# A decoder layer on one core: each feed-forward stage in three SBUF regions, its plain chunks first, and fixed PSUM banks

## The chip, the cores and the metric

The kernel runs on one core of one Trainium2 chip. The metric is device time in microseconds (us) of one execution. Profiles are of single executions; all times inside a trace count from the start of its span.

## What is computed

One layer of a hybrid decoder, batch 1, 256 tokens, model width 2048, all in float32:

```python
x = layer_norm(ALPHA * x + 0.5 * swiglu(x, ffn1_w_in, ffn1_w_out), ...)   # stage ffn1
z = x @ mix_w_in                                                          # stage hgrn
...                                                                       # convolution and gated recurrence
merged = sigmoid(gate_conv) * (y_conv @ branch_w_conv) + sigmoid(gate_hgrn) * (y_hgrn @ branch_w_hgrn)
x = layer_norm(ALPHA * x + merged @ mix_w_out, ...)                       # stage merge
x = layer_norm(ALPHA * x + 0.5 * swiglu(x, ffn2_w_in, ffn2_w_out), ...)   # stage ffn2
x = layer_norm(ALPHA * x + sigmoid(x @ ple_w_gate) * (p @ ple_w_proj), ...)  # stage ple
def swiglu(x, w_in, w_out):
    a, u = split(x @ w_in, 2); return (silu(a) * u) @ w_out
```

The hidden width of a feed-forward stage is 5504: ten chunks of 512 and one of 384.

## The kernel before

**Products.** Every float32 matrix product is made of three passes of TensorE (PE). A weight tile `raw` of 2x128 rows and 512 columns (512 KB) comes from HBM; ScalarE (ACT) rounds it to `wh` (the cast L884), VectorE (DVE) subtracts to get the rest `wl` (L895). Activations are split likewise into `xh`, `xl` (helper `halves`, L242 and L243). The passes wh·xh, wl·xh and wh·xl (L951 to L953) add up in a PSUM bank `acc`. Before they can be split, activations are transposed on PE into a PSUM tile `tp` (L232). A pair (`wh`, `wl`) is used for both token halves, t = 0 and t = 1.

**Units and quads.** A `Unit` is one block of 512 output columns: it goes over the inner dimension in blocks and through both token halves. A chunk of a feed-forward stage needs two units (gate and up columns). A chunk of full width can instead be a `Quad`: both column blocks and both token halves together by a scheme with seven instead of eight block products, in 2 steps; part of its weights are sums of loaded tiles, which DVE makes (L878) in a second ring of loads, `sraw`. A quad needs seven PSUM banks, `p1` to `p7`, and sums and differences of the plain transposed activations `yT`, made once by `sums` (`sh`, `sl`). In each feed-forward stage chunk 0 and the narrow chunk 10 are units, chunks 1 to 9 are quads. The chunks go in parts of 2, 2, 2, 2 and 3; after each chunk of a part from the second on come two output units of the part before (product with `w_out`), and the last four output units come at the end.

**What sets the order.** `feed` runs each time a pair has been used up: it starts loads as long as the rings have room (4 `raw`, 5 `sraw`), then casts and splits. 6 pairs are held, and more in a stage where EXTRA says so. Loads go through the queue of SyncE (SP) in the order in which they are written. `defer` runs a piece of code some ticks later, a tick being one pair's use for one token half. The instructions so written are then ordered for each engine by the framework's scheduler, which works from times of its own; each engine works through its list in that order.

**Regions.** `open_region(kind)` opens a stage's own memory: a pool on the left for its tiles, a pool `high` on the right for `sraw` and `yT`, and, where the numbers of banks differ (BANKS), new PSUM pools: 7 banks for accumulators and 1 for transposes in the feed-forward stages, else 4 accumulators, 2 for transposes and 2 for the recurrence.

**Between stages.** `layer_norm` (statistics, the square root L327 on ACT, four normalising operations L378 on DVE, transposes, then four ACT operations L370 that apply gain and bias into `y` or `yT`, then the split) stands between the stages: 8 operands, one for each of 4 columns blocks (c) and 2 token halves. Gain and bias are applied to `x` itself later (`affine_rows`, L353 and L354), at 40 to 100 ticks, with two loads `gb` into a slot of the `raw` ring.

**The start.** All eight loads of `x` are queued first with four of weights between them; then all eight transposes, each followed by its split and by an ACT copy to `yT` (L930), are written ahead of the first product.

Of the kernel before, what the change touches and what calls it, by code (L numbers as in the profile page):

```python
# [10 lines left out]
F32 = mybir.dt.float32  # L11
# [19 lines left out]
LONG = (12, 4)  # L31
EXTRA = {"ffn1": 0, "hgrn": 0, "merge": 0, "ffn2": 0, "ple": 1}
NSRAW = 5
BANKS = {"ffn1": (7, 1, 0), "ffn2": (7, 1, 0)}
ALPHA = 2.0 ** 0.25
# [71 lines left out]
def hybrid_layer(ctx: ExitStack, tc: tile.TileContext, x, p, ln_g, ln_b, ffn1_w_in, ffn1_w_out, mix_w_in,  # L107
# [16 lines left out]
    held = {}  # L124

    def open_region(kind):

        if "ctx" in region:
            region.pop("ctx").close()
        region["ctx"] = ExitStack()  # L130
        region["kind"] = kind
        held.update(sraw=0, freed=0)
        region["pool"] = region["ctx"].enter_context(tc.tile_pool(name=kind, bufs=1, side="left", reuse_waits="tile"))
        region["high"] = region["ctx"].enter_context(tc.tile_pool(name=kind + "h", bufs=1, side="right", reuse_waits="tile"))
        banks = BANKS.get(kind, (4, 2, 2))
        if banks != region.get("banks"):
            if "psum" in region:
                region["psum"].close()
            region["psum"] = ExitStack()
            region["banks"] = banks  # L140
            for n, b in zip("ath", banks):
                if b:
                    region[n] = region["psum"].enter_context(
                        tc.tile_pool(name="ps_" + n, bufs=b, space=PSUM, reuse_waits="tile"))

    def rtile(shape, dtype=F32, **kw):
        return region["pool"].tile(shape, dtype, **kw)

    def ptile(kind, name):
        return region[kind].tile([P, CC], F32, tag="bank", name=name)  # L150

# [7 lines left out]
    def defer(delay, fn):  # L159
        insort(later, (state["tick"] + delay, fn), key=lambda e: e[0])  # L160
# [67 lines left out]

    def transposed(src, nb, kind="t"):
        tp = ptile(kind, "tp")  # L230
        for i in range(nb):
            state["turned"] = nc.tensor.transpose(tp[:, i * P : (i + 1) * P], src[:, i * P : (i + 1) * P], ident).ins  # L232
        return tp
# [44 lines left out]
    def sums(stat):  # L278
# [30 lines left out]
        for i, fn in enumerate((third, first, second, fourth, lambda: delta(2), lambda: delta(3))):  # L309
            defer(2 + 2 * i, fn)  # L310

# [47 lines left out]
    def layer_norm(t, i, scale, stat):  # L359
# [3 lines left out]
        def operand(c, xc):  # L363
            y = plain_tile(t, c) if stat is x2 else st.tile([P, CC], F32, tag="silu", name="y", bufs=2)
            tp = transposed(xc, 4, "a" if stat is x2 else "t")
            if t == 0 and c < 2:
                gate["pe"] = state["turned"], 1
            for a in range(4):
                k = i * 16 + 4 * c + a
                nc.scalar.activation(y[:, a * P : (a + 1) * P], tp[:, a * P : (a + 1) * P], AF.Identity,  # L370
                                     bias=gbT[:, 48 + k : 49 + k], scale=gbT[:, k : k + 1])
# [555 lines left out]
    def first_operand(t, c):  # L927
        tp = transposed(xt[t][:, c * CC : (c + 1) * CC], 4, "a")
        halves(x0, t, c, tp, 4, "x")
        nc.scalar.copy(plain_tile(t, c), tp)  # L930
        if (t, c) == (NT - 1, 3):
            sums(x0)

    for c in range(4):
        for t in range(NT):
            load_x(t, c)
            defer(0, lambda t=t, c=c: first_operand(t, c))
            if c < 2:
                weight_dma()
# [98 lines left out]
```

## Time and profile before

| | us |
|---|---|
| median of 3 runs | 2266.34 (2264.94 to 2268.58) |
| profiled execution, its own time | 2265.55 |
| its span, first to last instruction | 2263.8 |
| busy PE, DVE, ACT within the span | 2215.5, 1682.0, 1130.7 |

The mean granted clock of TensorE was 0.992. A busy PE is not a PE at its peak: matmuls overlap, and their ends are modelled. For PE the number of instructions in a stretch tells more than the busy time: 128x512 matmuls that follow each other without a wait start about 0.23 us apart.

### The profile page before, as it was taken

The numbers are of one execution on the slowest core, as the hardware profiler recorded it, in microseconds if no ns is written. First come the engines' busy times: TensorE is split into PE (matmuls) and PEld (weight loads), VectorE is DVE, ScalarE is ACT, GpSimd is POOL, SyncE is SP. The second block draws the span as 40 slices with busy tenths as digits, with TensorE's granted clock in tenths as the row PEclk, the third lists the DMA queues.
The fourth block names the chain that finished last, engine by engine and source line by source line (L and its number), as shares of the span: only waits on it lengthen the run. The fifth ranks groups of instructions, "written<-read, shape, count | busy, mean of one in ns | idle before, by whom it ended". The sixth has DMA issues, their size and how long they took to land.

```text
span 2263.8 us, 26974 instructions
## 1 busy us (share of the span) xinstructions
PE 2215.5 (98%) x10110; PEld 1842.7 (81%) x10110; DVE 1682.0 (74%) x1944; ACT 1130.7 (50%) x1331; POOL 10.0 (0%) x32
## 2 busy tenths in 40 slices
PE   9999999999999999999999999899999999999997
PEld 7878888888897888888888888676888888889786
DVE  6888888888755678567445875778888898885667
ACT  5555555545545534444434443744555455554472
POOL 1000000000000000000000000000000000000000
PEclk9999999999999999999999999999999999999999
DMA  8566665666464565555555656556666666665554
GB/s 286 159 214 211 203 187 188 187 207 206 149 196 144 186 203 169 183 161 153 191 194 184 199 189 202 180 173 190 207 199 191 207 205 194 206 192 190 179 191 142
DMA packets 225337, 430.00 MB, mean 190 GB/s; under 512 B 13741, under 2 KB 22453, under 8 KB 225205
## 3 DMA queue, kind: packets, MB, share of 16 engines
q1 hardware_dynamic: 225204, 428.27, 59.6%
q8 instruction: 79, 1.29, 0.2%
q14 instruction: 54, 0.43, 0.1%
HBM read 426.12 MB, written 2.10 MB: 189 GB/s over the span
## 4 chain that ended last, share of the span: by engine, by line
PE 89%; DVE 4%; DMA 3%; ACT 2%; issue 1%; SPq 0%; DVEq 0%; ACTq 0%
PE acc L951 20%; PE acc L953 20%; PE acc L952 20%; PE p L952 9%; PE p L953 9%; PE p L951 9%; DVE wl L895 2%; PE tp L232 2%; DMA sraw<-in_ffn_w_in_dram 1%; PE gp L587 1%; DVE sraw L878 1%; ACT wh L884 1%; ACT yT L370 1%; DMA raw<-in_ple_w_gate_dram 0%; DMA raw<-in_ffn_w_in_dram 0%
## 5 line engine op out<-in xcount | busy, mean ns | idle before, releaser
L895 DVE TENSOR_TENSOR wl<-raw,wh 128x1024 fp32r<-128x1024 f32 (+2 forms) x660 | 787.4, 1201 | 285.7 <-ACT wh L884 264.9
L884 ACT CAST wh<-raw 128x1024 fp32r<-128x1024 f32 (+2 forms) x660 | 680.5, 1034 | 585.3 <-PE acc L953 407.5
L951 PE MATMUL acc<-wh,xh 128*128 128x512 f32 (+1 forms) x1088 | 418.9, 388 | 13.4 <-ACT xh L242 9.0
L953 PE MATMUL acc<-wh,xl 128*128 128x512 f32 (+1 forms) x1088 | 419.3, 386 | 0.1
L952 PE MATMUL acc<-wl,xh 128*128 128x512 f32 (+1 forms) x1088 | 418.2, 385 | 0.0
L884 ACT CAST wh<-sraw 128x1024 fp32r<-128x1024 f32 x252 | 262.7, 1049 | 286.9 <-DVE sraw L878 89.5
L895 DVE TENSOR_TENSOR wl<-sraw,wh 128x1024 fp32r<-128x1024 f32 x252 | 306.2, 1221 | 109.2 <-ACT wh L884 105.5
L952 PE MATMUL acc<-wl,gh 128*128 128x512 f32 x880 | 344.2, 391 | 0.9 <-DVE wl L895 0.9
L953 PE MATMUL acc<-wh,gl 128*128 128x512 f32 x880 | 343.3, 391 | 0.0
L951 PE MATMUL acc<-wh,gh 128*128 128x512 f32 x880 | 341.1, 392 | 0.0
L951 PE MATMUL p<-wh,xh 128*128 128x512 f32 x648 | 251.7, 391 | 3.9 <-ACT wh L884 3.9
L952 PE MATMUL p<-wl,xh 128*128 128x512 f32 x648 | 253.3, 391 | 0.8 <-DVE wl L895 0.8
L953 PE MATMUL p<-wh,xl 128*128 128x512 f32 x648 | 253.1, 391 | 0.0
L951 PEld LDWEIGHTS acc<-wh,xh 128*128 128x128 f32 x1088 | 205.4, 189 | 50.8 <-ACT xh L242 9.6
L953 PEld LDWEIGHTS acc<-wh,xl 128*128 128x128 f32 x1088 | 205.2, 189 | 38.8 <-DVE xl L243 1.4
L952 PEld LDWEIGHTS acc<-wl,xh 128*128 128x128 f32 x1088 | 205.5, 189 | 36.7
L952 PEld LDWEIGHTS acc<-wl,gh 128*128 128x128 f32 x880 | 165.4, 188 | 34.7 <-DVE wl L895 1.3
L953 PEld LDWEIGHTS acc<-wh,gl 128*128 128x128 f32 x880 | 165.4, 188 | 34.1
L951 PEld LDWEIGHTS acc<-wh,gh 128*128 128x128 f32 x880 | 165.3, 188 | 33.7
L878 DVE TENSOR_TENSOR sraw<-sraw 128x1024 f32<-128x1024 f32 x144 | 175.4, 1218 | 0.6
L952 PE MATMUL p<-wl,sh 128*128 128x512 f32 x432 | 169.3, 392 | 2.0 <-DVE wl L895 2.0
L953 PE MATMUL p<-wh,sl 128*128 128x512 f32 x432 | 168.8, 391 | 0.0
(187 smaller groups left out, 1847.7 us busy)
## 6 DMA issues: line engine op xcount, KB each, us to landing
raw<-in_ffn_w_in_dram SPq DMA_DIRECT2D x176, 512.0 KB, 4.6
raw<-in_mix_w_in_dram SPq DMA_DIRECT2D x176, 512.0 KB, 4.7
raw<-in_ffn_w_out_dram SPq DMA_DIRECT2D x168, 512.0 KB, 4.9
sraw<-in_ffn_w_in_dram SPq DMA_DIRECT2D x144, 512.0 KB, 4.6
raw<-in_mix_w_out_dram SPq DMA_DIRECT2D x32, 512.0 KB, 5.4
raw<-in_ple_w_gate_dram SPq DMA_DIRECT2D x32, 512.0 KB, 4.7
raw<-in_ffn_w_in_dram SPq DMA_DIRECT2D x32, 384.0 KB, 4.1
raw<-in_branch_w_conv_dram SPq DMA_DIRECT2D x16, 512.0 KB, 5.0
```

The costliest lines, as they stand in the source:

```text
L232: state["turned"] = nc.tensor.transpose(tp[:, i * P : (i + 1) * P], src[:, i * P : (i + 1) * P], ident).ins
L370: nc.scalar.activation(y[:, a * P : (a + 1) * P], tp[:, a * P : (a + 1) * P], AF.Identity, bias=gbT[:, 48 + k : 49 + k], scale=gbT[:, k : ...
L587: nc.tensor.matmul(gp[:, (h * 2 + t) * 64 : (h * 2 + t + 1) * 64], kd[:, h, t * P : (t + 1) * P], qd[:, h, t, :], start=True, stop=True)
L878: nc.vector.tensor_tensor(out=raw[:, :n, :w], in0=raw[:, :n, :w], in1=raws[el["add"]][:, :n, :w], op=ALU.add)
L884: nc.scalar.copy(h[:, :n, :w], raw[:, :n, :w])
L895: nc.vector.tensor_tensor(out=l[:, :n, :w], in0=raw[:, :n, :w], in1=h[:, :n, :w].bitcast(F32), op=ALU.subtract)
L951: nc.tensor.matmul(acc, sh, wh[:, a, :n], start=first, stop=False)
L952: nc.tensor.matmul(acc, sh, wl[:, a, :n], start=False, stop=False)
L953: nc.tensor.matmul(acc, sl, wh[:, a, :n], start=False, stop=last)
```

## The change

Seven things are changed, all in one kernel:

- A feed-forward stage has three regions: `lead` (chunk 0, with 3 more pairs), `ffn` (chunk 1 up to the last quad), `tail` (the last four output units, with 4 more pairs). The pool `high` is opened with `lead` and closed with `tail`.
- The two plain chunks come first: chunk 0 is 512 wide, chunk 1 is 384, chunks 2 to 10 are quads.
- `sums` runs when region `ffn` opens, ahead of chunk 1, no longer right after the last operand.
- The eight PSUM banks are one fixed tile each; a role (accumulators, transposes, recurrence) is a list of banks, handed out anew at every region, longest unused first; within a role, too, the bank longest unused is taken.
- The transposes for `ffn2` use the two banks of that role in `lead`, no longer the seven accumulators.
- The transposes of `x` at the start are deferred by 0 to 12 ticks.
- The copy to `yT` at the start is made by DVE instead of ACT.

```diff
-EXTRA = {"ffn1": 0, "hgrn": 0, "merge": 0, "ffn2": 0, "ple": 1}
+EXTRA = {"lead1": 3, "ffn1": 0, "tail1": 4, "hgrn": 0, "merge": 0, "lead2": 3, "ffn2": 0, "tail2": 4, "ple": 1}
-BANKS = {"ffn1": (7, 1, 0), "ffn2": (7, 1, 0)}
...
+        if kind.startswith("tail"):
+            region.pop("hctx").close()
+        region["pool"] = reopen("ctx", kind, "left")
         region["kind"] = kind
+        if kind.startswith("lead"):
+            region["high"] = reopen("hctx", kind + "h", "right")
+            held.update(sraw=0, freed=0)
+        if kind.startswith("ffn"):
+            roles = {"a": 7, "t": 1}
+        else:
+            roles = {"t": 2, "a": 4, "h": 2}
+        free = deque(sorted(banks, key=lambda n: used_at[n]))
+        for role, n in roles.items():
+            role_of[role] = [free.popleft() for _ in range(n)]
...
+    ps = pool("ps", space=PSUM)
+    banks = {n: ps.tile([P, CC], F32, tag=f"bank{n}", name=f"bank{n}") for n in range(8)}
+    used_at = {n: n for n in banks}
+    def ptile(role, name):
+        n = min(role_of[role], key=lambda n: used_at[n])
+        used_at[n] = max(used_at.values()) + 1
+        return banks[n]
...
-            defer(2 + 2 * i, fn)
+            defer(1 + 2 * i, fn)
...
-            tp = transposed(xc, 4, "a" if stat is x2 else "t")
+            tp = transposed(xc, 4)
...
-            if stat is x2 and (t, c) == (NT - 1, 3):
-                sums(stat)
...
+        starts = [0, CC] + [DFF - (11 - ch) * CC for ch in range(2, 12)]
-            c0 = ch * CC
-            w = min(CC, DFF - c0)
-            if w == CC and ch > 0:
+            c0 = starts[ch]
+            w = starts[ch + 1] - c0
+            if ch > 1:
...
+                if ch == 1:
+                    units.append(("ffn" + name, lambda: sums(xs)))
                 in_units(ch, gs[pi], ci)
...
+        units.append(("tail" + name, lambda: None))
         for c in range(4):
             out_unit(len(parts) - 1, c)
...
-        tp = transposed(xt[t][:, c * CC : (c + 1) * CC], 4, "a")
+        tp = transposed(xt[t][:, c * CC : (c + 1) * CC], 4)
         halves(x0, t, c, tp, 4, "x")
-        nc.scalar.copy(plain_tile(t, c), tp)
-        if (t, c) == (NT - 1, 3):
-            sums(x0)
+        nc.vector.tensor_copy(plain_tile(t, c), tp)
...
-            defer(0, lambda t=t, c=c: first_operand(t, c))
+            defer((0, 1, 3, 5, 7, 10, 8, 12)[2 * c + t], lambda t=t, c=c: first_operand(t, c))
```

The amount of work stays as it was: 9946 instructions on PE, 861 loads on SP and the same matmuls by shape; DVE has the 8 copies to `yT` that ACT no longer has, and ACT has one more load of a function table.

How the order of the instructions moves, at the places of which the prediction speaks (in the changed kernel the lines of the helpers are L243 for L232, L253 and L254 for L242 and L243, L897 and L908 for L884 and L895, L962 to L964 for L951 to L953, L338 for L327, L381 for L370, L868 for L855; banks are called `bank_79` to `bank_86`, and the halves of `x` are `x_83`, `x_84` before and `x_94`, `x_95` now).

PE at the start of the program. Before, the last two of the eight groups of transposes and the first passes:

```order
L232 MATMUL tp<-ident,x_83 128x128 x4
L232 MATMUL tp<-ident,x_84 128x128 x4
L951 MATMUL acc<-wh,xh 128x512
L952 MATMUL acc<-wl,xh 128x512
L953 MATMUL acc<-wh,xl 128x512
```

Now, from the first transposes on:

```order
L243 MATMUL bank_79<-ident,x_94 128x128 x4
L243 MATMUL bank_80<-ident,x_95 128x128 x4
L962 MATMUL bank_82<-wh,xh 128x512
L963 MATMUL bank_82<-wl,xh 128x512
L962 MATMUL bank_83<-wh,xh 128x512
L963 MATMUL bank_83<-wl,xh 128x512
L964 MATMUL bank_82<-wh,xl 128x512
L962 MATMUL bank_82<-wh,xh 128x512
L963 MATMUL bank_82<-wl,xh 128x512
L964 MATMUL bank_82<-wh,xl 128x512
L243 MATMUL bank_79<-ident,x_94 128x128 x4
```

The first pass stands behind two groups of transposes instead of eight; the other six stand between passes.

SP's queue of loads around the first quads of `ffn1` (`sraw` loads belong to quads, four for a step; `in_ffn_w_out` to output units). Before:

```order
L855 DMA raw<-in_ffn_w_in_dram 128x2x512 x10
L855 DMA sraw<-in_ffn_w_in_dram 128x2x512 x2
L855 DMA raw<-in_ffn_w_in_dram 128x2x512 x2
L855 DMA sraw<-in_ffn_w_in_dram 128x2x512 x2
L855 DMA raw<-in_ffn_w_in_dram 128x2x512 x2
```

Now:

```order
L868 DMA sraw<-in_ffn_w_in_dram 128x2x512 x4
L868 DMA raw<-in_ffn_w_in_dram 128x2x384 x7
L868 DMA raw<-in_ffn_w_in_dram 128x2x512 x6
L868 DMA sraw<-in_ffn_w_in_dram 128x2x512 x2
L868 DMA raw<-in_ffn_w_in_dram 128x2x512 x2
L868 DMA sraw<-in_ffn_w_in_dram 128x2x512 x2
L868 DMA raw<-in_ffn_w_out_dram 128x2x512 x2
L868 DMA sraw<-in_ffn_w_in_dram 128x2x512 x2
L868 DMA raw<-in_ffn_w_out_dram 128x2x512
```

Before, 17 `sraw` loads, those of two quads and one more, are queued ahead of the first load of an output unit. Now it is 9, those of one quad and one more, and the narrow chunk's loads stand ahead of the quad's.

ACT between `ffn1` and `hgrn`, from the square root of the first token half on. Before:

```order
L327 ACTIVATE r<-w 128x1
L884 CAST wh<-raw 128x1024 x2
L370 ACTIVATE y<-tp,gbT 128x128 x4
L242 CAST xh<-y 128x512
L884 CAST wh<-raw 128x1024 x2
L370 ACTIVATE y<-tp,gbT 128x128 x4
```

Now:

```order
L338 ACTIVATE r<-w 128x1
L897 CAST wh<-raw 128x1024 x3
L381 ACTIVATE y<-bank_80,gbT 128x128 x4
L381 ACTIVATE y<-bank_85,gbT 128x128 x4
L253 CAST xh<-y 128x512
L554 ACT_TABLE_LOAD
L554 ACTIVATE both<-both 128x16
L253 CAST xh<-y 128x512
```

One cast more stands ahead of the first `y`, and none between the first and the second.

ACT between `merge` and `ffn2`, likewise. Before:

```order
L327 ACTIVATE r<-w 128x1
L884 CAST wh<-raw 128x1024 x5
L370 ACTIVATE yT<-tp,gbT 128x128 x4
L242 CAST xh<-yT 128x512
L327 ACTIVATE r<-w 128x1
```

Now:

```order
L338 ACTIVATE r<-w 128x1
L897 CAST wh<-raw 128x1024 x3
L381 ACTIVATE yT<-bank_81,gbT 128x128 x4
L381 ACTIVATE yT<-bank_85,gbT 128x128 x4
L897 CAST wh<-raw 128x1024
L253 CAST xh<-yT 128x512
```

Three casts instead of five stand ahead of the first `yT`; a fourth now stands between it and the first `xh`.

More of the change, by code (lines that the diff above doesn't have):

```diff
@@ L124, in hybrid_layer, with reopen @@
     held = {}
+    def reopen(part, name, side):
+        if part in region:
+            region.pop(part).close()
+        region[part] = ExitStack()
+        return region[part].enter_context(tc.tile_pool(name=name, bufs=1, side=side, reuse_waits="tile"))
     def open_region(kind):
-        if "ctx" in region:
-            region.pop("ctx").close()
-        region["ctx"] = ExitStack()
+        if kind.startswith("tail"):
+            region.pop("hctx").close()
+        region["pool"] = reopen("ctx", kind, "left")
         region["kind"] = kind
[L132 to L144, printed above, removed]
+        if kind.startswith("lead"):
[8 more added lines that the diff above has]
+            role_of[role] = [free.popleft() for _ in range(n)]
     def rtile(shape, dtype=F32, **kw):
         return region["pool"].tile(shape, dtype, **kw)
-    def ptile(kind, name):
-        return region[kind].tile([P, CC], F32, tag="bank", name=name)
+    ps = pool("ps", space=PSUM)
+    banks = {n: ps.tile([P, CC], F32, tag=f"bank{n}", name=f"bank{n}") for n in range(8)}
+    used_at = {n: n for n in banks}
+    role_of = {}
+    def ptile(role, name):
+        n = min(role_of[role], key=lambda n: used_at[n])
+        used_at[n] = max(used_at.values()) + 1
+        return banks[n]
     state = {"tick": 0}
@@ L226, in hybrid_layer, with transposed @@
         masks[b] = m
-    def transposed(src, nb, kind="t"):
-        tp = ptile(kind, "tp")
+    def transposed(src, nb):
+        tp = ptile("t", "tp")
         for i in range(nb):
@@ L396, in hybrid_layer, with ffn @@
     units = []
-    def ffn(xs, w_in, w_out, ln_i, nxt):
+    def ffn(name, xs, w_in, w_out, ln_i, nxt):
         parts = [range(0, 2), range(2, 4), range(4, 6), range(6, 8), range(8, 11)]
+        starts = [0, CC] + [DFF - (11 - ch) * CC for ch in range(2, 12)]
         gs = [Stat() for _ in parts]
@@ L464, in out_unit @@
             chunks, last = parts[pi], pi == len(parts) - 1
-            row = chunks[0] * CC
-            nk = min(DFF - row, len(chunks) * CC) // P
+            row = starts[chunks[0]]
+            nk = (starts[chunks[-1] + 1] - row) // P
             def epi_o(t, acc):
@@ L494, in hybrid_layer @@
     w1i, w1o = ffn1_w_in[0], ffn1_w_out[0]
-    units.append(("ffn1", lambda: None))
-    ffn(x0, w1i, w1o, 0, x1)
+    units.append(("lead1", lambda: None))
+    ffn("1", x0, w1i, w1o, 0, x1)
     wm = mix_w_in[0]
@@ L781, in hybrid_layer @@
         units.append(Unit(ms, mix_w_out[0], 0, 16, c * CC, CC, epi_m, split=LATE if c == 3 else SPLIT))
-    units.append(("ffn2", lambda: None))
-    ffn(x2, ffn2_w_in[0], ffn2_w_out[0], 2, x3)
+    units.append(("lead2", lambda: None))
+    ffn("2", x2, ffn2_w_in[0], ffn2_w_out[0], 2, x3)
     pst = Stat()
@@ L1008, in hybrid_layer @@
     region.pop("ctx").close()
-    region.pop("psum").close()
 _INS = ['x', 'p', 'ln_g', 'ln_b', 'ffn1_w_in', 'ffn1_w_out', 'mix_w_in', 'conv_w', 'hg_lower_bound', 'hg_norm_w',
```

## The prediction

> **What bounds it now.** I read the page first (busy time, then the groups of instructions), then PE's own table of stretches for its instruction counts, then PE, ACT and DVE in order of time wherever PE's count falls behind.
>
> ```profile
> PE 2215.5 (98%) x10110; PEld 1842.7 (81%) x10110; DVE 1682.0 (74%) x1944; ACT 1130.7 (50%) x1331; POOL 10.0 (0%) x32
> ```
>
> PE is the bound, and the change leaves its work as it is. So the question is how much time PE loses, and where. The stretches of PE (length, busy time, instructions, granted clock, share of the DMA engines, GB/s):
>
> ```profile
> 0.00:16.30 16.30, 10.69 (x44) 1.00 0.88 300
> 102.00:142.00 40.00, 37.25 (x164) 1.00 0.54 169
> 142.00:205.60 63.60, 63.60 (x286) 1.00 0.66 208
> 711.40:732.10 20.70, 15.25 (x66) 0.84 0.48 152
> 1424.00:1447.40 23.40, 14.49 (x67) 0.78 0.41 134
> 1523.50:1577.00 53.50, 47.84 (x191) 0.94 0.54 166
> 1577.00:1585.00 8.00, 7.11 (x31) 1.00 0.89 307
> 2139.00:2161.50 22.50, 18.38 (x81) 0.92 0.57 189
> ```
>
> The third row is one quad with two output units in the steady state: 63.60/286 = 0.2224 us per instruction and no idle time. Against that pace the others lose: second quad of ffn1 40.0 − 164×0.2224 = 3.5 us; second quad of ffn2 53.5 − 42.5 = 11.0, and 1.1 in the row below, so 12.1; and the three passages between stages (711, 1424 and 2139 us), where a lower clock adds to the idle time. Before 16.3 us no product runs at all. These six places are all that the change reaches; the orders of DVE and ACT between them are the same.
>
> **The start.** PE, then ACT and DVE:
>
> ```profile
> 4.51 1.12 PE L232 MATMUL tp<-ident,x 128*128 128x128 f32 x4
> 6.78 1.11 PE L232 MATMUL tp<-ident,x 128*128 128x128 f32 x4 [1.16 <-DMA x<-in_x_dram]
> 12.99 3.68 PE L232 MATMUL tp<-ident,x 128*128 128x128 f32 x16 [0.92 <-DMA x<-in_x_dram]
> 16.32 0.78 PE L951 MATMUL acc<-wh,xh 128*128 128x512 f32 x1
> 17.46 0.40 PE L951 MATMUL acc<-wh,xh 128*128 128x512 f32 x1
> 709.59 0.63 PE L232 MATMUL tp<-ident,x 128*128 128x128 f32 x4
> 7.93 0.59 ACT L242 CAST xh<-tp 128x512 fp32r<-128x512 f32 x1 [0.64 <-PE tp L232]
> 6.84 1.23 DVE L895 TENSOR_TENSOR wl<-raw,wh 128x1024 fp32r<-128x1024 f32 x1 [6.84 <-ACT wh L884]
> 13.04 0.68 DVE L243 TENSOR_TENSOR xl<-tp,xh 128x512 fp32r<-128x512 f32 x1
> ```
>
> Everything that the first pass needs is there long before 16.32: the second group of transposes ends at 7.9, its `xh` at 8.5, the first `wl` at 8.1. Now the first pass starts at about 7.7, behind two groups. It cannot run at full pace. PE is still slow: the 16 transposes from 12.99 start 3.33/16 = 0.21 us apart, and four take 1.12 where a later group takes 0.63, so PE ran at half rate up to the first products, although the column says 1.00; rows below (716.65 to 717.08) show a pass of 0.43 then, instead of 0.2224. Six groups of transposes, 0.44 us each at full rate, now lie between the passes. And DVE has 8 `wl` at 1.2, 8 `xl` and 8 copies to `yT` at 0.6 to make for the first unit: 19 us. Pass by pass: half rate from 7.7 to about 12.5 (some 4.5 us of work, as in 12.99 to 17.46; 14 passes and a group), then 82 passes and five groups, 18.2 + 2.2, with 1 us lost to `wl`: the unit ends near 34 instead of 16.32 + 96×0.2224 = 37.7. Gain 4; at best 6.5 (no half rate), at worst 2. The copies moved to DVE are 4.8 of those 19 us, which the 26 from 7.7 to 34 cover.
>
> **The quads.** Two quads in a row run DVE dry, because a step's `sraw` loads wait for slots and DVE's sums for both. The waits of PE in the second quad of ffn2, and DVE's splits of `sraw` in the stretch 102 to 142 us:
>
> ```profile
> PE p L951 <- ACT wh L884: 3.9, 6, 2.1
> PE p L952 <- DVE wl L895: 1.8, 3, 0.9
> L895 DVE TENSOR_TENSOR wl<-sraw,wh 128x1024 fp32r<-128x1024 f32 x12 | 14.6, 1220 | 4.4 <-ACT wh L884 4.4
> ```
>
> Now each quad, the first included, is followed by two output units or the tail, which is the pattern of the row 142.00:205.60, that loses nothing. In ffn1 all 3.5 come back. In ffn2 gain and bias are applied meanwhile, at ticks 44, 64, 84 and 104: before, the second and third fell into the second quad; now the plain chunks take 64 ticks, so two sets fall ahead of the quads, one (4 DVE operations of 0.68, a slot of `raw`) into the first quad, one into the output units. The first quad of ffn2 had one such set before and lost little. `sums` moves beside chunk 1: DVE then has 16 narrow `wl` (19.5 us at most), 6 `sl` (4.1) and in ffn2 two sets (5.4) beside 192 narrow passes (0.75×0.2224 each, 32 us); hidden, with little room. SP's loads are the same 861, and POOL is not touched. I leave 1.1: gain 11, between 9 and 12.1. Casts for the tail's extra pairs are written only when the tail opens, but the order shows them among the last quad's closing operations, 8 `wl` ahead of its last product; I count nothing there, and 1.5 per stage if that cover fails.
>
> **ffn1 to hgrn.** ACT, DVE, PE:
>
> ```profile
> 706.71 1.28 ACT L327 ACT_TABLE_LOAD   x1
> 708.00 0.20 ACT L327 ACTIVATE r<-w 128x1 f32<-128x1 f32 x1
> 708.11 1.98 ACT L884 CAST wh<-raw 128x1024 fp32r<-128x1024 f32 x2
> 715.59 1.04 ACT L884 CAST wh<-raw 128x1024 fp32r<-128x1024 f32 x1 [3.18 <-DMA raw<-in_mix_w_in_dram]
> 721.77 0.20 ACT L327 ACTIVATE r<-w 128x1 f32<-128x1 f32 x1 [0.82 <-DVE w L326]
> 708.89 1.92 DVE L378 TENSOR_SCALAR x<-x,mv,r 128x512 f32<-128x512 f32 x4
> 710.72 4.62 DVE L895 TENSOR_TENSOR wl<-raw,wh 128x1024 fp32r<-128x1024 f32 x4
> 716.09 0.76 PE L951 MATMUL acc<-wh,xh 128*128 128x512 f32 x1 [4.41 <-DVE x L475]
> 716.65 0.63 PE L952 MATMUL acc<-wl,xh 128*128 128x512 f32 x1
> 717.08 0.63 PE L953 MATMUL acc<-wh,xl 128*128 128x512 f32 x1
> ```
>
> ACT stands behind casts whose loads were started late (each waits for a `wl` from 710.72 on to free a slot), and the first pass waits for a bank that the other half's sum (L475) still reads. With the tail's pairs three more splits are done before the statistics, so those loads are early, and the banks are others. From the rows: three casts from 708.11 end at 711.1, two groups of four `y` (1.5 each) at 714.1, the first `xh` at 714.6. On DVE `xl` follows three `wl` (1.15 each), the sum and the statistics: 716.7. So the first pass comes 1.5 earlier, the third 0.5; but the second operand comes some 4 us earlier (it stood behind the cast at 715.59), and the second half's square root at 718.0 (with a table load of 1.28 in between) instead of 721.77: 3.8. The later passes hang on that root. Gain 3.8, between 1 and 5.5.
>
> **merge to ffn2.**
>
> ```profile
> 1419.13 2.93 ACT L884 CAST wh<-raw 128x1024 fp32r<-128x1024 f32 x3
> 1426.71 1.05 ACT L884 CAST wh<-raw 128x1024 fp32r<-128x1024 f32 x1 [4.64 <-DMA raw<-in_ffn_w_in_dram]
> 1429.32 1.04 ACT L884 CAST wh<-raw 128x1024 fp32r<-128x1024 f32 x1 [1.57 <-DMA raw<-in_ffn_w_in_dram]
> 1430.27 1.50 ACT L370 ACTIVATE yT<-tp,gbT 128x128 f32<-128x128 f32 x4
> 1433.70 1.91 DVE L378 TENSOR_SCALAR x<-x,mv,r 128x512 f32<-128x512 f32 x4
> 1435.91 0.78 PE L953 MATMUL acc<-wh,xl 128*128 128x512 f32 x1
> ```
>
> Two casts that wait for loads hold up `yT`. Now both groups of `yT` stand ahead of them: 1423.9 to 1426.9; the fourth cast, at the same landing, ends at 1427.9, `xh` at 1428.4, four us earlier. But `xl` now stands behind the `wl` of the fifth cast (1430.4): 1432.2, and the third pass 3.7 earlier than 1435.91. Then it turns: DVE normalises the second half behind two more `wl` and `xl`, about 1435.9 instead of 1433.70, and with two banks its transposes wait for `yT`. So 2 of the 4 go back: gain 2, between −2 and 4.
>
> **ffn2 to ple.**
>
> ```profile
> 2145.89 1.05 ACT L884 CAST wh<-raw 128x1024 fp32r<-128x1024 f32 x1 [3.53 <-DMA raw<-in_ple_w_gate_dram]
> 2148.97 1.50 ACT L370 ACTIVATE y<-tp,gbT 128x128 f32<-128x128 f32 x4
> 2150.52 1.11 PE L232 MATMUL tp<-ident,x 128*128 128x128 f32 x4 [2.64 <-ACT y L370]
> ```
>
> PE's transposes wait for the bank that an earlier `y` frees, and the second `y` stands behind two casts that wait for loads, the first of them shown. Now one stands there, `y` comes at about 2147.1, and PE has the short products with `ple_w_proj` to run meanwhile, which also go ahead of the last output passes. Gain 3, between 0 (as late as before) and 5.
>
> **Sum.** 4 + 3.5 + 11 + 3.8 + 2 + 3 = 27.3 from the profiled 2265.55 (its span 2263.8 and 1.75 around it): 2238.2. The median stands 0.8 above that execution, within the runs' spread, so I forecast 2238. The lower ends sum to 2 + 3 + 9 + 1 − 2 + 0 = 13 (2252), the upper to 6.5 + 3.5 + 12.1 + 5.5 + 4 + 5 = 36.6 (2229).
>
> [...] In the trace PE was at half rate through all transposes, 3.3 us of them back to back, and rose 1.1 us after the first products. [...]
>
> **Rivals.**
> - *The passages give nothing*: the waits in front of `y` and `yT` are replaced by those for two transpose banks (all four groups of one half now stand ahead of the first pass, the third waiting for the first `y`). For it: 2150.52 shows such a wait, 2.64 us. Against: the casts that wait for loads are fewer at all three. Time 2238.2 + 8.8 = 2247.
> - *The quads still run dry*, because of the set in the first quad of ffn2 and fewer loads ahead: half of 14.5 is lost, 2245. Against: the steady row with nothing lost.
> - *The clock stays at half rate through the first unit*: 82 passes × 0.2 and the transposes' 2.2 more, 18.6 us: 2257, the start slower than before. Against: PE has little to wait for once it starts, and the clock of 0.84 over the 20.7 us from 711.4 leaves at most 6.6 us of half rate, idle time included.
> - *Slower*: fixed banks tie a quad's first passes to readers of the quad or units before. A wait for a bank is in the trace: 4.41 us at 716.09. 18 quads lie in the two stages, so the gain of 27.3 is gone at 1.5 us for each, and slower by 0.2% from 1.8. At 2.6 it would be 2238.2 + 47 = 2285. Against: seven banks taken in turn is what the pools did too, and the row 142.00:205.60 has no wait at all.
>
> **How the numbers follow.** The forecast 0.68, its own range 2229 to 2249; passages 0.12; quads 0.07; half rate 0.06; slower 0.03; no change in sum 0.03; 0.01 for better than the upper ends. The range 2227 to 2251 leaves out half rate, no change and slower, and a little beside, about 0.14. 0.2% (4.5 us) is about what a measurement of this kernel can tell from no change; faster by that is 0.94, same 0.03, slower 0.03.
>
> **What would show it.** The first L962 at 7 to 9 us; passes 0.43 apart until 12 to 14; the first unit over by 36; no PE wait above 1 us in the first quads; the first pass of hgrn some 5 us after the last one of ffn1, not 5.3 and slow; the cast counts before `yT` as ordered. Wrong if slow passes last beyond 20 us, if ACT waits for `raw` ahead of `y` as long as now, or if a bank's wait shows up in every quad.

## The result, and the profile after

The changed kernel takes 2227.49 us (median of 4 runs, 2225.86 to 2229.26), the kernel before beside it 2266.70 (2264.94 to 2268.58): a ratio of 0.9827, 95% interval 0.981 to 0.9844. The forecast was 2238, range 2227 to 2251. So the sign and the places were right, and the gain was larger than the sum's 27.3: 39 us between the medians, 37.0 between the profiled executions (2228.56 now, its span 2226.7). The median lies 0.5 us inside the range.

The page's line on busy time, and the longest waits of PE (who waits, for whom: us in total, times, longest):

```profile
PE 2203.0 (99%) x10110; PEld 1837.0 (82%) x10110; DVE 1685.6 (76%) x1952; ACT 1127.8 (51%) x1324; POOL 10.0 (0%) x32
```

```profile
PE bank L243 <- DMA x<-in_x_dram: 2.1, 1, 2.1
PE bank L243 <- ACT yT L381: 2.0, 2, 1.2
PE bank L938 <- POOL ident masks.py:199: 1.6, 1, 1.6
PE bank L243 <- ACT y L381: 1.4, 2, 1.2
PE bank L962 <- ACT xh L253: 0.9, 1, 0.9
PE bank L964 <- DVE xl L254: 0.7, 1, 0.7
```

Before, PE waited 9.0 us for `xh` and 5.2 for the sum L475; now no wait is above 1.3 but the two at the program's start, for `x` and for the constant `ident`. The stretches that answer to those of the prediction (length; busy time and instructions of PE, then of PEld, DVE, ACT and POOL; the granted clock, DMA share, GB/s):

```profile
0.00:16.30 16.30, 12.54 (x48) 10.11 (x49) 8.34 (x10) 7.51 (x9) 5.74 (x28) 1.00 0.84 293
153.80:194.40 40.60, 40.60 (x181) 33.64 (x180) 35.64 (x35) 22.50 (x24) 0.00 (x0) 1.00 0.67 209
704.40:725.10 20.70, 19.54 (x92) 14.86 (x91) 11.31 (x29) 20.03 (x44) 0.00 (x0) 1.00 0.16 53
1410.40:1433.80 23.40, 19.84 (x92) 15.68 (x90) 20.12 (x33) 20.56 (x46) 0.00 (x0) 0.93 0.62 202
1558.60:1602.00 43.40, 42.89 (x190) 34.83 (x188) 38.28 (x38) 22.36 (x25) 0.00 (x0) 1.00 0.60 190
2106.00:2128.50 22.50, 21.42 (x103) 16.88 (x102) 17.88 (x29) 19.11 (x39) 0.00 (x0) 1.00 0.75 259
```

Second quads (rows 2 and 5) now run without idle time, or with half a microsecond of it. In 20.7 us behind `ffn1` PE does 92 instructions where it did 66, and at full clock; in 23.4 us behind `merge` 92 instead of 67; in 22.5 us behind `ffn2` 103 instead of 81.

Where the time went is seen best by the start of the same pass in both traces, from PE's rows in order of time. Both kernels have done the same work on PE at each of these marks:

| mark | before | after | earlier by | since the mark above |
|---|---|---|---|---|
| 96th pass (end of the first unit) | 38.35 | 35.54 | 2.8 | 2.8 start |
| last pass of ffn1 | 710.51 | 703.54 | 7.0 | 4.2 quads of ffn1 |
| 96th pass of hgrn | 744.89 | 731.34 | 13.6 | 6.6 ffn1 to hgrn |
| last pass of merge | 1423.04 | 1409.48 | 13.6 | 0 |
| 96th pass of ffn2 | 1460.49 | 1440.91 | 19.6 | 6.0 merge to ffn2 |
| seventh last output pass of ffn2 | 2138.56 | 2107.58 | 31.0 | 11.4 quads of ffn2 |
| 96th pass of ple | 2183.34 | 2147.41 | 35.9 | 4.9 ffn2 to ple |
| last pass | 2248.62 | 2212.68 | 35.9 | 0 |
| end of the span | 2263.8 | 2226.7 | 37.1 | 1.2 |

The last line is no work of the change: from the last pass to the end it is 14.0 us here and 14.0 to 14.1 in the profiles of all twelve experiments, one of them nearly the kernel before; only the profile of before has 15.2, the excess behind its last DVE instruction.

### The profile page after: what moved, and what is told of

Its sections match the earlier page's. It is cut to its first block, busy times and chain, and to the rows that moved or that the text cites. A ratio compares the mean times of both kernels' runs of the same rounds, so it can differ in the third digit from the quotient of the medians.

```text
span 2226.7 us, 26935 instructions
## 1 busy us (share of the span) xinstructions
PE 2203.0 (99%) x10110; PEld 1837.0 (82%) x10110; DVE 1685.6 (76%) x1952; ACT 1127.8 (51%) x1324; POOL 10.0 (0%) x32
## 4 chain that ended last, share of the span: by engine, by line
PE 92%; DVE 4%; DMA 2%; ACT 1%; issue 1%; SPq 0%; DVEq 0%; ACTq 0%
PE bank L962 30%; PE bank L964 29%; PE bank L963 29%; DVE wl L908 2%; PE bank L243 2%; PE bank L600 1%; DVE sraw L891 1%; DMA raw<-in_ffn_w_in_dram 1%; ACT wh L897 0%; DMA sraw<-in_ffn_w_in_dram 0%; DMA gb<-in_ln_g_dram 0%; DMA x<-in_x_dram 0%; DMA raw<-in_ffn_w_out_dram 0%; DVE x L400 0%; DVE x L401 0%
## 5 line engine op out<-in xcount | busy, mean ns | idle before, releaser
L908 DVE TENSOR_TENSOR wl<-raw,wh 128x1024 fp32r<-128x1024 f32 (+2 forms) x660 | 788.6, 1203 | 262.8 <-ACT wh L897 245.4
L897 ACT CAST wh<-raw 128x1024 fp32r<-128x1024 f32 (+2 forms) x660 | 680.4, 1035 | 581.5 <-PE bank L964 410.1
L964 PE MATMUL bank<-wh,xl 128*128 128x512 f32 (+1 forms) x1736 | 670.9, 387 | 0.7 <-DVE xl L254 0.7
L963 PE MATMUL bank<-wl,xh 128*128 128x512 f32 (+1 forms) x1736 | 671.0, 387 | 0.0
L962 PE MATMUL bank<-wh,xh 128*128 128x512 f32 (+1 forms) x1736 | 669.6, 388 | 1.3 <-ACT xh L253 0.9
L897 ACT CAST wh<-sraw 128x1024 fp32r<-128x1024 f32 x252 | 262.5, 1050 | 273.1 <-PE bank L964 120.3
L908 DVE TENSOR_TENSOR wl<-sraw,wh 128x1024 fp32r<-128x1024 f32 x252 | 306.1, 1223 | 102.5 <-ACT wh L897 98.8
L964 PEld LDWEIGHTS bank<-wh,xl 128*128 128x128 f32 x1736 | 327.0, 188 | 64.5 <-DVE xl L254 2.4
L962 PEld LDWEIGHTS bank<-wh,xh 128*128 128x128 f32 x1736 | 327.1, 188 | 63.9 <-ACT xh L253 1.7
L963 PEld LDWEIGHTS bank<-wl,xh 128*128 128x128 f32 x1736 | 327.0, 188 | 61.8 <-DVE wl L908 0.2
L963 PE MATMUL bank<-wl,gh 128*128 128x512 f32 x880 | 343.9, 391 | 0.0
L964 PE MATMUL bank<-wh,gl 128*128 128x512 f32 x880 | 342.9, 391 | 0.0
L962 PE MATMUL bank<-wh,gh 128*128 128x512 f32 x880 | 341.9, 392 | 0.0
L964 PEld LDWEIGHTS bank<-wh,gl 128*128 128x128 f32 x880 | 165.4, 188 | 34.1
L962 PEld LDWEIGHTS bank<-wh,gh 128*128 128x128 f32 x880 | 165.3, 188 | 33.8
L964 PE MATMUL bank<-wh,sl 128*128 128x512 f32 x432 | 168.5, 390 | 0.0
L962 PE MATMUL bank<-wh,sh 128*128 128x512 f32 x432 | 164.9, 390 | 0.5 <-ACT wh L897 0.5
L962 PEld LDWEIGHTS bank<-wh,sh 128*128 128x128 f32 x432 | 81.1, 188 | 17.9 <-ACT wh L897 1.4
```

Of the source, the lines that this page charges most:

```text
L897: nc.scalar.copy(h[:, :n, :w], raw[:, :n, :w])
L908: nc.vector.tensor_tensor(out=l[:, :n, :w], in0=raw[:, :n, :w], in1=h[:, :n, :w].bitcast(F32), op=ALU.subtract)
L962: nc.tensor.matmul(acc, sh, wh[:, a, :n], start=first, stop=False)
L963: nc.tensor.matmul(acc, sh, wl[:, a, :n], start=False, stop=False)
L964: nc.tensor.matmul(acc, sl, wh[:, a, :n], start=False, stop=last)
```

## The experiments

Each run's profile is read by the same marks. The medians come from four sessions; the ratios below are against the kernel before in the same session (2265.2 to 2266.9). Three columns belong to the start and the quads, three to a passage: from the last pass of the stage before to the first and to the 96th of the next (for ple from the seventh last output pass of ffn2 to its 96th). "Slow" counts, where two banks serve the transposes there, the passes that start 0.38 to 0.47 us apart at the head of ffn2.

```
                       time     first  96th   ffn1    hgrn        ffn2              ffn2     ple
                       median   pass   pass   quads   1st  96th   1st  96th  slow   quads    96th
before                 2266.70  16.32  38.35  672.2   5.58 34.38  9.43 37.45         678.1   44.77
changed                2227.49   8.57  35.54  668.0   2.94 27.80  5.46 31.43   6     666.7   39.83
e1  order alone        2244.47  17.16  38.79  667.9   3.60 32.06  9.02 35.88         666.2   43.42
e2  no tail pairs      2230.64   7.27  33.58  668.0   1.25 31.54  5.33 32.42  11     665.6   39.79
e3  fixed banks        2234.43   7.53  34.08  668.0   1.48 34.59  5.33 32.83  13     665.7   40.92
e4  start together     2228.86   7.40  34.20  668.0   2.94 27.79  5.37 31.35   5     667.4   40.97
e5  start two banks    2227.52   7.53  33.19  668.2   2.94 27.83  5.34 32.34  11     665.5   39.91
e6  start undone       2231.78  10.25  37.95  667.5   2.94 27.82  5.45 32.17  10     668.5   39.22
e7  lead2 four banks   2230.04   7.51  33.90  668.0   2.94 27.81  9.09 34.51         665.8   39.33
e8  lead2 one bank     2229.66   7.53  32.78  668.0   2.94 27.81  5.29 32.71         667.3   39.57
e9  warm products      2225.40   7.27  34.05  668.0   2.94 27.81  6.58 31.12   0     665.3   39.35
e10 warm transposes    2226.02   7.31  33.97  668.0   2.94 27.78  5.42 30.82   0     666.3   40.03
e11 no tail region     2231.72   7.36  33.64  668.0   1.25 30.88  5.34 32.73  13     665.4   41.17
e12 no lead pairs      2228.94   7.45  33.68  668.1   2.94 27.83  5.35 32.84  12     668.2   39.75
```

A passage of unchanged order repeats to 0.05 us at hgrn and scatters by 1.5 at ffn2, 3 in the quads of ffn2 and 1.8 at ple; differences smaller than that are not read. The times of one kernel scatter by 3 to 4 us, so differences of under 2 us between medians aren't read either.

**The chunk order alone**, in the kernel before.

```diff
+        starts = [0, CC] + [DFF - (11 - ch) * CC for ch in range(2, 12)]
-            c0 = ch * CC
-            w = min(CC, DFF - c0)
-            if w == CC and ch > 0:
+            c0 = starts[ch]
+            w = starts[ch + 1] - c0
+            if ch > 1:
```

> The kernel before, with the chunk order alone changed (the two plain chunks first); regions, pairs, PSUM pools and the start are as before. Theory A (each part has its own place): the dry quads in ffn1 (4.3 us between the two profiles) and in ffn2 (11.4 us) come back, the three passages and the start stay as they were: 2266.5 - 15.7 = 2251, first product at 16.3, first pass of hgrn 5.6 us after the last of ffn1. Rival B (the longer last output unit, 12 blocks of the inner dimension instead of 11, is what shortens the passages, since half 0 is summed earlier): hgrn and ple are entered up to 6.2 and 4.9 us sooner too: 2240. Rival C (the quads also need the extra pairs and the sums beside chunk 1): the quads give half of 15.7 or less: 2259 or more.

Ratio 0.9904 (0.989 to 0.9919), 21.3 us of the 39. Both stages' quads come back whole (4.3 and 11.8 us), with 6 pairs, the old pools and `sums` at its old place: rival C falls. Beyond theory A the passages give 2.3, 1.6 and 1.4; so the longer last output unit of rival B, which can act at hgrn and ple alone, is worth 3.7 us at most, where it was to give 11.

**Without the tail's extra pairs.**

```diff
-"tail1": 4 ... "tail2": 4
+"tail1": 0 ... "tail2": 0
```

> The changed kernel without the 4 extra pairs of the two tail regions. Theory A (these pairs empty ACT and DVE ahead of the statistics and so give the passages to hgrn and to ple): 6.2 + 4.9 = 11 us are lost there and nothing elsewhere: 2238.5, with ACT's square root again behind casts and PE idle for over 3 us ahead of hgrn. Rival B (the last output unit of 12 blocks does it): under 2 us lost: 2227 to 2229.5.

Between the two: hgrn loses 3.7 (31.54 against 27.80), ple nothing; ratio 0.9843 (0.9828 to 0.9858). What is lost shows on ACT, in order of time, of the changed kernel and then of e2:

```profile
696.96 0.20 ACT L338 ACTIVATE r<-w 128x1 f32<-128x1 f32 x1 [7.74 <-DVE w L337]
...
701.86 1.05 ACT L897 CAST wh<-raw 128x1024 fp32r<-128x1024 f32 x1 [0.31 <-PE bank L964]
702.82 3.10 ACT L381 ACTIVATE y<-bank,gbT 128x128 f32<-128x128 f32 x8
705.80 0.63 ACT L253 CAST xh<-y 128x512 fp32r<-128x512 f32 x1
...
707.86 0.60 ACT L253 CAST xh<-y 128x512 fp32r<-128x512 f32 x1
...
709.77 0.20 ACT L338 ACTIVATE r<-w 128x1 f32<-128x1 f32 x1
```

```profile
697.10 0.20 ACT L338 ACTIVATE r<-w 128x1 f32<-128x1 f32 x1
...
704.85 1.05 ACT L897 CAST wh<-raw 128x1024 fp32r<-128x1024 f32 x1 [0.66 <-DMA raw<-in_mix_w_in_dram]
707.03 1.05 ACT L897 CAST wh<-raw 128x1024 fp32r<-128x1024 f32 x1 [1.13 <-DMA raw<-in_mix_w_in_dram]
707.98 0.61 ACT L253 CAST xh<-y 128x512 fp32r<-128x512 f32 x1
```

With the pairs the second `xh` is there 4.3 us behind the last pass of `ffn1` (703.54), without them 6.4 behind it (701.58), since two casts that wait for loads stand in front, as in the kernel before.

**Banks by number.**

```diff
-        free = deque(sorted(banks, key=lambda n: used_at[n]))
-        for role, n in roles.items():
-            role_of[role] = [free.popleft() for _ in range(n)]
+        free = deque(sorted(banks))
+        for role in "ath":
+            role_of[role] = [free.popleft() for _ in range(roles.get(role, 0))]
```

> The changed kernel, but every region hands out the same PSUM banks by number (7 accumulators and 1 for transposes in the quads' region, elsewhere 4, 2 and 2) instead of the ones longest unused; within a role the longest unused is still taken. Theory A (in the passages the chain is ACT and DVE, the banks are off it): within 2 us of the changed kernel, 2226 to 2229.5. Rival D (before, the first pass of hgrn waited 4.41 us for a bank that the last sum still read; other banks are what removed that): 4 us or more lost, most of it at hgrn and ple: 2231 or more.

Ratio 0.986 (0.9843 to 0.9876); 34.59 at hgrn, as bad as before the change, so theory A falls there. But rival D's mechanism is not seen either: the first pass comes early (1.48), and no pass waits for a sum. ACT and PE of e3:

```profile
703.57 0.81 ACT L381 ACTIVATE y<-bank,gbT 128x128 f32<-128x128 f32 x2
704.39 1.28 ACT L554 ACT_TABLE_LOAD   x1
...
705.81 2.19 ACT L381 ACTIVATE y<-bank,gbT 128x128 f32<-128x128 f32 x6
708.01 1.28 ACT L338 ACT_TABLE_LOAD   x1
...
709.42 1.12 ACT L253 CAST xh<-y 128x512 fp32r<-128x512 f32 x2
...
710.07 0.50 PE L962 MATMUL bank<-wh,xh 128*128 128x512 f32 x1 [2.29 <-ACT xh L253]
```

With other banks the scheduler wrote another order: two table loads and the third `y` now stand ahead of the second `xh`, and PE waits 2.29 us for it. The banks act through ACT's order. Whether a true wait for a bank or the scheduler's reckoning of one made that order, this run doesn't separate.

**The start.** e4 sets all eight delays to 0; e5 also takes the copies to `yT` back to ACT; e6 also gives transposes and accumulators seven common banks in the first region.

```diff
-            defer((0, 1, 3, 5, 7, 10, 8, 12)[2 * c + t], lambda t=t, c=c: first_operand(t, c))
+            defer(0, lambda t=t, c=c: first_operand(t, c))
```

```diff
-        nc.vector.tensor_copy(plain_tile(t, c), tp)
+        nc.scalar.copy(plain_tile(t, c), tp)
```

```diff
+        if kind == "lead1":
+            role_of["a"] = role_of["t"] = role_of["t"] + role_of["a"] + role_of["h"][:1]
```

> The changed kernel with all eight transposes of x written ahead of the first product again (delays 0); the copy to yT stays on DVE. Theory A (the spread alone gives the 2.9 us of the first unit): first product at 15.5 to 16.5 us, 96th pass near 38.3 instead of 35.5, time 2230.4. Rival E (the gain is the copy's move off ACT, or is made up by the second unit): under 1 us lost, 2228.5 or less.

> The changed kernel with the delays at 0 and the copy to yT back on ACT, so that of the three edits at the start only the two banks for transposes are left. Theory F (the two banks alone spread the transposes, since a third group can't start before the first is read): first product at 7 to 8.5 us, 96th pass at 33.5 to 35.5, time 2227 to 2229.5. Rival G (the copies matter: 8 of some 0.6 us on ACT, 4.8 us more ahead of casts and halves): 96th pass at 36.5 or later, 2230 or more.

> As the run before, and in the first region transposes and accumulators share seven banks as they did before the change: all that spreads the transposes is undone. In the written order the first product now stands behind three groups, the first twelve passes belong to half 0, and five groups stand together behind them. Theory F: 96th pass at 36.5 to 38.5, some 3 us lost against the run before, 2231. Rival E (the gain at the start does not hang on the banks either): 96th pass before 36, under 1 us lost.

Ratios 0.9832 (0.9817 to 0.9846), 0.9829 (0.9815 to 0.9844) and 0.9846 (0.9832 to 0.9861). Theory A falls: without the delays the first product still comes at 7.40, and with the copies on ACT at 7.53. With seven banks it comes at 10.25, five groups stand together, and the 96th pass is at 37.95, 4.8 later than in e5, as theory F had it:

```profile
10.25 0.79 PE L964 MATMUL bank<-wh,xh 128*128 128x512 f32 x1 [0.51 <-ACT yT L945]
...
14.58 2.35 PE L245 MATMUL bank<-ident,x 128*128 128x128 f32 x20
```

So the delays in the diff, and the move of the copies, bring nothing that can be seen; that transposes have two banks of their own spreads them.

**Four banks, and one, for the transposes ahead of ffn2.**

```diff
-            roles = {"t": 2, "a": 4, "h": 2}
+            roles = {"t": 4, "a": 4} if kind == "lead2" else {"t": 2, "a": 4, "h": 2}
```

For one bank, `{"t": 1, "a": 4, "h": 2}` in the same place.

> The changed kernel, with four PSUM banks instead of two for the transposes ahead of ffn2 (the two of the recurrence, which that region doesn't use). Theory H (ACT's order sets this passage; with four banks all four yT of half 0 stand ahead of the first xh, 2 groups of 1.45 us more): PE waits for no bank, but the first pass comes 2.5 to 3 us later, 8 us instead of 5.5 behind the last of merge, and the half rate behind it stays: 2230. Rival I (as the prediction had it, the transposes' waits for yT's bank, 1.22 and 0.74 us, are the price of two banks): 2 us won, 2225.5, no half rate.

> The changed kernel, with one PSUM bank instead of two for the transposes ahead of ffn2. On ACT the first xh then stands behind one group of yT and a cast, not two groups and a cast. Theory H: the first pass of ffn2 comes 1.4 us earlier, the second operand later by 1 to 2 us; the passage's loss stays within 1 us of the 6.4 of the changed kernel: 2226.5 to 2228.5. Rival I (waits for banks are the price): 2 us or more lost: 2229.5 or more.

Four banks: 9.09 to the first pass, nearly the 9.43 of before, and 34.51 to the 96th, 1.7 to 3.2 later than with two; ratio 0.9841 (0.9824 to 0.9857). Theory H holds, rival I has the wrong sign. PE and ACT of the changed kernel, then of e7:

```profile
1411.96 0.66 PE L243 MATMUL bank<-ident,x 128*128 128x128 f32 x4 [1.22 <-ACT yT L381]
1413.36 0.66 PE L243 MATMUL bank<-ident,x 128*128 128x128 f32 x4 [0.74 <-ACT yT L381]
1414.94 0.50 PE L962 MATMUL bank<-wh,xh 128*128 128x512 f32 x1 [0.93 <-ACT xh L253]
...
1416.35 0.80 PE L964 MATMUL bank<-wh,xl 128*128 128x512 f32 x1 [0.67 <-DVE xl L254]
...
1410.41 2.90 ACT L381 ACTIVATE yT<-bank,gbT 128x128 f32<-128x128 f32 x8 [1.90 <-PE bank L243]
1413.32 1.05 ACT L897 CAST wh<-raw 128x1024 fp32r<-128x1024 f32 x1
1414.28 0.61 ACT L253 CAST xh<-yT 128x512 fp32r<-128x512 f32 x1
```

```profile
1408.08 1.91 PE L243 MATMUL bank<-ident,x 128*128 128x128 f32 x16
1416.93 0.80 PE L962 MATMUL bank<-wh,xh 128*128 128x512 f32 x1 [6.95 <-ACT xh L253]
...
1408.77 2.90 ACT L381 ACTIVATE yT<-bank,gbT 128x128 f32<-128x128 f32 x8 [1.90 <-PE bank L243]
1412.53 2.90 ACT L381 ACTIVATE yT<-bank,gbT 128x128 f32<-128x128 f32 x8
...
1416.22 0.66 ACT L253 CAST xh<-yT 128x512 fp32r<-128x512 f32 x1
```

Where nothing holds the transposes back, all four are written first, ACT applies gain and bias to all four, and the first `xh` stands behind them. One bank (ratio 0.9837, 0.9822 to 0.9852) leaves the passage as it is, 32.71; but the first pass did not come 1.4 us earlier as I expected, since the cast ahead of `xh` then waits 1.24 us for its load, which landed 3.6 us behind the last pass of `merge` (3.8 in the changed kernel).

**Filling PE's waits.** A constant is multiplied or transposed into a spare bank behind the second, third and fourth group of transposes; nobody reads it.

```diff
+            if stat is x2 and t == 0 and c:
+                with tc.issue_after(state["turned"]):
+                    warm = ptile("h", "warm")
+                    for _ in range((0, 9, 5, 7)[c]):
+                        nc.tensor.matmul(warm[:, :P], ident, ident, start=True, stop=True)
```

In e10 the last line is `nc.tensor.transpose(warm[:, :P], ident, ident)`.

> The changed kernel with 21 matmuls of 128x128 on a constant, whose result nobody reads, in the waits of PE between merge and ffn2 (9, 5 and 7 of some 0.11 us behind the second, third and fourth group of transposes; the waits are 1.22, 0.74 and 0.93 us). Theory L (half rate follows idle time of some 3 us within a few us): the passes of ffn2 start 0.23 us apart from the first on, where now 8 of them take 0.43; the first pass is not delayed; the passage's loss falls from 6.4 to 4.8 us, time 2226. Rival M (something else slows the first passes of a stage): the same 8 slow passes, 6.3 to 7.4 as in the runs so far.

> As the run before, with 21 transposes of a constant 128x128 in place of the matmuls. Theory L with transposes counting as work: the same as there, a loss of 4.8 us in the passage. Rival N: transposes do not count, so the 8 slow passes stay and the loss is 6.3 to 7.4. [...]

The slow passes are gone in both, where the eight other runs with two banks there have 5 to 13. First e10, then the changed kernel, PE at the head of ffn2:

```profile
1413.29 0.50 PE L967 MATMUL bank<-wh,xh 128*128 128x512 f32 x1
...
1414.73 0.50 PE L969 MATMUL bank<-wh,xl 128*128 128x512 f32 x1 [0.71 <-DVE xl L254]
1415.06 0.40 PE L967 MATMUL bank<-wh,xh 128*128 128x512 f32 x1
1415.30 0.39 PE L968 MATMUL bank<-wl,xh 128*128 128x512 f32 x1
1415.53 0.40 PE L969 MATMUL bank<-wh,xl 128*128 128x512 f32 x1
```

```profile
1416.94 0.63 PE L962 MATMUL bank<-wh,xh 128*128 128x512 f32 x1
1417.37 0.63 PE L963 MATMUL bank<-wl,xh 128*128 128x512 f32 x1
1417.79 0.63 PE L964 MATMUL bank<-wh,xl 128*128 128x512 f32 x1
```

So theory L holds in that the slow passes go with the waits (6 in the changed kernel, none with either fill), and rivals M and N fall; how busy PE was ahead of each fall of the clock stands in the last section. In time it is little: the 96th pass stands at 30.82 and 31.12 against 31.35 to 32.84 (mean 32.3), some 1.3 us, and the ratios, 0.9824 (0.9809 to 0.9839) and 0.9823 (0.9808 to 0.9837), can't be told from the changed kernel's. Each matmul of e9 became two instructions of 0.11 us, so its fill was twice as long as meant and put off the first pass by 1.2.

**No tail region; no pairs in the lead.**

```diff
-        units.append(("tail" + name, lambda: None))
-        if kind.startswith("tail"):
+        if kind in ("hgrn", "ple"):
```

```diff
-"lead1": 3 ... "lead2": 3
+"lead1": 0 ... "lead2": 0
```

> The changed kernel without the region tail at all: no extra pairs there, and the pools of the quads are closed only when hgrn or ple opens, as before the change. Theory J (only the pairs matter, as their removal alone showed): hgrn's passage loses 6.9 instead of 3.4 us, ple's stays at 2.4: 2231. Rival K (closing the pools early is what lets ple's loads and tiles come in time; removing the pairs alone did not touch that): ple's passage loses 5 to 7 us again: 2234 or more.

> The changed kernel without the 3 extra pairs of the lead regions. Theory O (the pairs let casts and splits run ahead while yT and xh are made; they are what is left of the gain at merge to ffn2, since four banks cost 3.1 of 6.0 us there): the passage loses 9.4 instead of 6.4 us, 2230.5. Rival P (they do nothing there, since the casts wait for loads): 6.3 to 7.4 us, time within 1 us of the changed kernel.

Without the region, hgrn loses 3.1 and ple is at 41.17, 0.2 above the other runs: theory J, ratio 0.9852 (0.9836 to 0.9869). Without the lead's pairs ffn2's 96th pass is at 32.84, as in runs that have them: rival P, ratio 0.9837 (0.9822 to 0.9852). These pairs bring nothing that the marks show.

## Why the prediction was right, and where its sizes failed

- **Start, forecast 4, measured 2.8.** The mechanism is right: the first products run behind two groups of transposes, at half rate to 13.3 (0.43 us apart from 10.20 on, 0.23 from 13.72 on), with the other groups between them. What makes that order the prediction leaves open; my expectation for e4 put it down to the delays, and it is the two banks. The size is that of one execution. The second piece of `x` landed late there (a wait of 2.1 us, 1.1 in e5) and the first product came at 8.57:

```profile
7.81 1.12 PE L243 MATMUL bank<-ident,x 128*128 128x128 f32 x4 [2.09 <-DMA x<-in_x_dram]
8.57 0.78 PE L962 MATMUL bank<-wh,xh 128*128 128x512 f32 x1
...
13.48 0.40 PE L964 MATMUL bank<-wh,xl 128*128 128x512 f32 x1
```

  In the ten experiments that keep the two banks the first unit ends at 32.8 to 34.2, 4.1 to 5.6 before the old 38.35; 34 was forecast. The forecast's working has a slip that hid in this: 14 passes and a group don't fit into the 4.8 us from 7.7 to 12.5 at 0.43 us a pass, some 9 do, so by its own pace the unit would end near 35; and the old unit ended at 38.35, not at 37.7. In one of the ten, e5, half rate was over sooner: from 9.90 on its passes are 0.24 us apart.
- **Quads, forecast 3.5 and 11, measured 4.2 and 11.4.** Right, and by the step given: e1 shows that the order alone does it. The set of gain and bias in the first quad cost nothing that shows. The rival of dry quads is false, and so is the slower one: no bank's wait stands in any quad.
- **ffn1 to hgrn, forecast 3.8 (at most 5.5), measured 6.6.** The step that failed is the chain from ACT's rows of before: I kept the first square root where it was and put three casts behind it. It moved: 6.6 us ahead of the last pass of `ffn1` (696.96 to 703.54) instead of 2.5 (708.00 to 710.51). The last unit has 12 blocks, so half 0 is summed 8.5 us ahead, not 6.9, and ACT, idle for 7.74 us, stood ready. The order alone (e1) brings the root to 4.5 ahead, and so does e2, without the pairs; the pairs bring the rest. The second half's root, on which the forecast put its 3.8, came 5.0 earlier: 6.2 us behind the last pass of `ffn1` instead of 11.3. And I left out of the sum that the half rate there would go: the 9 passes from 716.09 on were 0.43 us or more apart, at a granted clock of 0.84 over the 20.7 us from 711.40, and now those from 707.55 on are 0.23 apart, at 1.00 over the 20.7 from 704.40. (The sign "some 5 us after the last one of ffn1, not 5.3" didn't follow from the sum either: before it was 5.58, less 1.5 is 4.1; measured 2.94.) Of the 6.6, the order alone brings 2.3 and the extra pairs 3.7; but e3 shows that another choice of banks loses it all, so these shares don't simply add.
- **merge to ffn2, forecast 2 (at most 4), measured 6.0.** The first `xh` came where it was forecast (1414.28, which is 1427.9 in the time of before, as `merge` ended 13.6 earlier; 1428.4 was written). "So 2 of the 4 go back" is the step that failed. The third pass came 6.0 earlier, not 3.7, as the fifth cast's load was no longer late, and DVE normalised the second half 1.1 earlier, not 2.2 later. And the two banks have the other sign: the transposes do wait for them, and that is what keeps `xh` in front (first pass at 5.46, with four banks at 9.09, before at 9.43). With four banks 2.9 of the 6.0 remain; the passes are then 0.23 us apart again 12.7 us behind the last pass of `merge` (1407.84 to 1420.56) instead of 14.2 (1423.04 to 1437.21), and what shortened that no run separates.
- **ffn2 to ple, forecast 3 (at most 5), measured 4.9.** The mechanism is as forecast: the second `y` stands behind one cast that waits for its load, not two, and comes 7.4 us behind the mark instead of 10.4 (8.5 was forecast); the wait of 2.64 and the half rate behind it are gone (a clock of 0.92 over the 22.5 us from 2139.0 before, 1.00 over those from 2106.0 now). In e1 two such casts still stand there (9.2); in e2, e3 and e11 it is one (6.5 to 7.1). So the order alone accounts for 1.4, the pairs for nothing and the region for little; e3 adds 1.1 at most, within the scatter. What takes the second cast away was not found.
- **Left out:** 1.2 at the end, an accident of the profile before; it is in the profiled 2265.55 from which the sum was made.

By mechanisms: the rivals *passages give nothing* and *half rate through the first unit* are false (27.80 instead of 34.38; full rate from 13.3). The range held, by 0.5 us, because its lower end stood just past all upper ends together; two of these, 5.5 and 4, were passed, and the start fell short of its forecast. That is luck as much as reckoning.

Open remain the rest at ple and merge, and what single fixed tiles do against pools that are closed and opened; the latter was not tried by itself. The diff also has an eighth edit beside the seven listed: `sums` makes its pieces at 1, 3, 5, ... ticks instead of 2, 4, 6, .... No run tries it alone; e1 is without it, and its quads come back whole.

## What to carry to other kernels

A scarce resource can be a good scheduler's brake: with two PSUM banks for transposes the products come between them, while with four (ahead of `ffn2`: first pass at 9.09 instead of 5.46) or seven (at the start, e6: 10.25 instead of the 7.53 of e5) more transposes run ahead and the work that the first product needs stands behind them; so try fewer banks before writing delays. Work that needs loads in bursts is best put between work that needs few: this chunk order alone was worth 21.3 us of the 39. And price an idle PE at its length plus the half-rate passes behind it: ahead of `ffn2` waits of 1.22, 0.74, 0.93 and 0.67 us stand in front of 6 passes that start 0.43 us apart, not 0.23; fills with 21 useless transposes (e10) left none of these.

## What the runs showed of the hardware

- Half rate stood behind stretches in which PE was idle for over half the time. The clock's record in the traces of before and of the changed kernel has five falls to 0.50 between its beginning and the last pass. Half rate then lasts 3.41, 6.83 or 10.24 us, one, two or three times 3.41; PE's busy time in the 3.41 us ahead of each:

| | at 0.50 | us | PE busy in the 3.41 us ahead |
|---|---|---|---|
| before, `hgrn` | 713.44 to 720.26 | 6.83 | 1.66 |
| before, `ffn2` | 1426.82 to 1437.06 | 10.24 | 0.46 |
| before, quads of `ffn2` | 1553.12 to 1559.94 | 6.83 | 1.42 |
| before, `ple` | 2150.45 to 2153.86 | 3.41 | 0.85 |
| now, `ffn2` | 1416.19 to 1419.61 | 3.41 | 1.39 |

  The wait ahead of `ple` is a single one of 2.64 us; ahead of `ffn2`, now, there are waits of 0.74, 0.93 and 0.67, of which 2.0 us lie in those 3.41. Behind the single wait of 1.16 us ahead of `hgrn`, now, the clock stays at 1.00, and so it does behind the 3.41 us from 1409.37, now, in which PE was busy for 2.03. In e3 waits of 1.16 and 0.74 us at the transposes of the second token half of `hgrn` lie in one such stretch, and the clock falls behind it (length, PE busy and instructions, granted clock, DMA):

```profile
717.78:721.19 3.41, 1.51 (x13) 1.00 0.00 0
721.19:724.60 3.41, 3.41 (x11) 0.50 0.00 0
```

  The same order of instructions ahead of ffn2 has 5 to 13 slow passes.
- Transposes in PE's waits did as well as products. In e10 21 transposes of a constant in the waits left no slow pass, just as products did in e9, against 6 in the changed kernel. At the start of e1 PE ran 16 transposes, and nothing else, in the 3.2 us ahead of the first product. They are 0.2 us apart, as at half rate before (four at full rate take 0.63); but the first two products are only 0.31 apart, and the second takes 0.40; in the changed kernel the first two (8.57 and 9.15) are 0.58 apart, and the second takes 0.63.

```profile
13.94 3.46 PE L232 MATMUL tp<-ident,x 128*128 128x128 f32 x16 [0.92 <-DMA x<-in_x_dram]
17.16 0.48 PE L952 MATMUL acc<-wh,xh 128*128 128x512 f32 x1
17.47 0.40 PE L953 MATMUL acc<-wl,xh 128*128 128x512 f32 x1
```

- The clock column reads 1.00 where the trace has no record: the first record begins at 13.3 us (17.1 before), and ahead of it passes are 0.43 us apart (10.20 to 11.90, now). From there on column and spacings agree: 0.93 over the 23.4 us from 1410.4 is the half rate from 1416.19 to 1419.61.
